# Decay's and gate's running sums as VectorE scans instead of TensorE products, in a one-core hybrid decoder layer

## The chip, the cores and the metric

The kernel runs on one core of one Trainium2 chip. The metric is the device time of one execution in microseconds (us), as a median over runs. The engines are named TensorE (PE in the profile; PEld are its weight loads), VectorE (DVE), ScalarE (ACT), GpSimd (POOL) and SyncE (SP, here the queue from which nearly all DMAs are issued).

## The reference

One decoder layer over 4096 tokens of width 1024. A modulated RMSNorm output h feeds one input projection; its columns go to three parallel mixers (sliding-window attention, RWKV-7, gated linear attention, "GLA"), each is multiplied by a SiLU gate path, and one output projection, a norm and a gate follow. The change is in how two mixers get their decays, cut here to that:

```python
# RWKV-7: per token and channel, state S of each 64-wide head
w = -softplus(-(w0 + tanh(xw @ w1) @ w2)) - 0.5
decay = exp(-exp(w))            # = exp(-e^-0.5 * sigmoid(w0 + ...))
S = S * decay[None, :] + sa[:, None] * (kk * a)[None, :] + v[:, None] * k[None, :]
y = S @ r
# GLA, 4 heads with 32 key and 64 value channels
gk = log_sigmoid((h @ gk1) @ gk2 + gk_b) / 16
b = cumsum(gk)                  # inside a chunk
o = masked((q * exp(b)) @ (k * exp(-b)).T) @ v + (q * exp(b)) @ S
S = exp(b_last) * (S + (k * exp(-b)).T @ v)
```

## The kernel before, in words

Two phases. In the first, 16 blocks of 256 tokens (NT) pass through stages that are written as generators: `stage_a` (norm, hT), `stage_p` (the projections pv, lp, zz, gqk), `stage_d` (named "w": gate and decay), `stage_qa`, `stage_qb`, `stage_qc` (RWKV's triangular systems inside a chunk and their inverse), `stage_v`, `stage_k`, `stage_r` (GLA's products), `stage_q2` (RWKV's chain of states, four chunks of 64 tokens a block), and `stage_c` and `stage_g`, which prepare the second phase's weights. The second phase does attention, gates and the output projection. Results of the first pass through DRAM (hscr, mscr).

The code's order comes from `emit`, which picks the stream whose inputs are ready first. `Order` records every step with an estimated cost and its dependencies, and `pin` lays the steps of each engine out in a fixed order: the step of lowest rank that is ready, on TensorE preferring the tiling of the array that is set. So all instructions have the line of one helper (`call`, L337), and a group in the profile is known by its tiles. Where a scan is among the steps, `Order.note` has a rate of its own for it in the changed kernel.

The names that matter:
- `gla_gate` (L598): zp is the transpose of the gate's 16 low-rank columns and a column of ones (vg[:, a, 256:273]); zlT its copy; gp the product with gk2 (gk2s); ga and gl the log-sigmoid.
- `stage_d`: cgp are gate's running sums, products of gl with a triangular table CTG that is counted from the middle of the 128 tokens; cgc, egp, egm their clamp and exponentials; gmax the largest sum met, for a flag that selects another path. uw is the tanh of the low-rank decay input, wps its product with w2 (w2s) plus w0, which comes in by extra bf16 products (one16 with w0p); aps the same for the rate a; gw and ta their tanh. cw are decay's running sums, products of gw with the table CT, also counted from a chunk's middle; ep and em their exponentials, 65 positions a chunk; cd and em0 what carries a state to the next chunk's and the next block's reference.
- `stage_q2`: Sst is the state, rescaled by em0 at a block's start (L1504). `stage_r`: Gpk and Gst are GLA's state, packed and spread.
- PSUM banks have tags. cw takes "at" and "tr", which the other stages' products use too; cgp takes "m".

The TensorE products in single precision run in two passes each, and small ones are laid on parts of the array: 64*64 means 64 rows by 64 columns.

Of the kernel before, what the change touches and what calls it, by code (L numbers as in the profile page):

```python
# [21 lines left out]
P = 128  # L22
D = 1024
T = 4096
NT = 256
# [5 lines left out]
GATE_LIMIT = 30.0  # L31
# [33 lines left out]
class Order:  # L65
# [34 lines left out]
    def note(self, eng, name, outs, ins, func, r):  # L100
# [44 lines left out]
        else:  # L145
# [256 lines left out]
def hybrid_kernel(ctx, tc, x, xc, rows, ada1, adaw, w1, wl, w2, wo, cst, abias, out):  # L402
# [238 lines left out]
    bdm, gk2s, sinks = kept[:, 0:256], kept[0:17, 256:384], kept[:, 384:392]  # L641


    with ExitStack() as p1:

        soon = ("tables", "scolb", "uw", "w0p0", "w0p1", "one16", "mu_s", "mu_c", "a0h")
        late = ("td", "tf0", "tf1", "Sst0", "Sst1", "lnx")
        tags = ("gvh", "gvl", "xh", "b1", "gl", "bl", "cs", "ch", "gw", "zs", "gaw", "gacc", "zl0", "zl1", "zl2", "early",
                "zb1", "ta", "em", "ep", "zb0", "b2", "zb2", "kg", "kt", "egm", "egp", "qg", "vg", "c2", "middle",
                "AS", "osb", "c3", "KB", "ATm", "c1", "RA", "UV", "BK", "cd", "em0", "bon", "ysb", "rs", "Ss", "lasts")  # L650
# [43 lines left out]
        tables = pp.tile([P, 771], F32, name="tables")  # L694
        masks = pp.tile([P, 3 * P + 32], F32, name="masks")
        w2s, a2s, w0s = tables[0:HD, 0:256], tables[:, 0:256], tables[0:HD, 256:512]
        CT, CTG = tables[:, 512:642], tables[:, 642:771]
# [169 lines left out]
        w0p = [pp.tile([HD, 256], BF16, name=f"w0p{j}") for j in range(2)]  # L867
        one16 = pp.tile([HD, HD], BF16, name="one16")
        V.memset(one16, 1.0)
        for j in range(2):  # L870
            V.tensor_copy(w0p[j], w0s)
            V.tensor_tensor(w0s, w0s, w0p[j], op=ALU.subtract)
            V.tensor_scalar(w0p[j], w0p[j], ident[0:HD, j : j + 1], None, op0=ALU.mult)
        V.tensor_add(w0p[0], w0p[0], w0p[1])
        V.scalar_tensor_tensor(w0p[1], w0s, ident[0:HD, 2:3], w0p[0], op0=ALU.mult, op1=ALU.add)
# [5 lines left out]
        gmax = cp.tile([P, 1], F32, name="gmax")  # L881
        G.memset(gmax, 0.0)
# [171 lines left out]
        def stage_p(i):  # L1054
# [56 lines left out]
            for b in range(2):  # L1111
# [5 lines left out]
            V.scalar_tensor_tensor(qg, gqk[:, 0:NT].rearrange("p (a n) -> p a n", a=2), gq_s, e["egp"][:, :, 1:129],  # L1117
                                   op0=ALU.mult, op1=ALU.mult)
            V.scalar_tensor_tensor(kg, gqk[:, NT : 2 * NT].rearrange("p (a n) -> p a n", a=2), Wt["gqk"][2],
                                   e["egm"][:, :, 1:129], op0=ALU.mult, op1=ALU.mult)  # L1120

        def stage_d(i):
# [7 lines left out]
            yield from gla_gate(vg, b1([17, NT], "zlT"), b1([P, NT], "ga"), gl, mt)  # L1130
            yield [gl, "m"]
# [3 lines left out]
            egp = wt([P, 2, 129], "egp", 2)  # L1135
            egm = wt([P, 2, 129], "egm", 2)
            e["egp"], e["egm"] = egp, egm
            cg3 = cgp[:, :258].rearrange("p (a n) -> p a n", a=2)
            cgc = wt([P, 2, 129], "cgc", tag="gl")
            V.tensor_scalar(cgc, cg3, -40.0, 40.0, op0=ALU.max, op1=ALU.min)  # L1140
            gm2 = st.tile([P, 2], F32, tag="gm2", name="gm2")
# [27 lines left out]
            yield [gw, "m", "tr"]  # L1169
            ep = wt([P, 2, 4, 65], "ep", 1)  # L1170
            em = wt([P, 2, 4, 65], "em", 1)
            e["ep"], e["em"] = ep, em
# [9 lines left out]
            joint(False)  # L1182
# [7 lines left out]
            em0 = wt([P, 2, 1], "em0", 2)  # L1190
            e["cd"], e["em0"] = cd, em0
# [16 lines left out]
        def stage_qa(i):  # L1208
# [18 lines left out]
            ta, ep, em = e["ta"], e["ep"], e["em"]  # L1227
# [14 lines left out]
            ems_ = em.rearrange("p b c n -> p (b c) n")[:, :, 1:65]  # L1242
# [139 lines left out]
        def stage_r(i):  # L1382
# [30 lines left out]
            for a in range(2):  # L1413
# [3 lines left out]
                V.scalar_tensor_tensor(heads4[0], now.rearrange("p (o n) -> p o n", o=1).to_broadcast([P, 4, HD]),  # L1417
# [647 lines left out]
    with tc.If(flag == 0):  # L2065
# [7 lines left out]
        with tc.For_i(0, NS, 1) as iv:  # L2073
# [5 lines left out]
            for a in range(2):  # L2079
                PE.transpose(pM[:, a * P : (a + 1) * P], fg[:, 0, a * P : (a + 1) * P], ident)  # L2080
# [159 lines left out]
```

## Time and profile before

| | |
|---|---|
| median of 3 runs | 2008.36 us (2005.95 to 2013.02) |
| profiled execution | 2010.31 us, span 2008.2 us, mean granted TensorE clock 0.989 |
| TensorE busy | 1915.3 us (95%), 24899 instructions |
| weight loads | 1481.6 us (74%) |
| VectorE busy | 1498.6 us (75%), 4246 instructions |
| ScalarE busy | 1130.5 us (56%) |
| GpSimd busy | 311.9 us (16%) |
| DMA | 258.77 MB, mean 129 GB/s |

A group's row in the profile reads: line, engine, operation, written tile <- read tiles, shapes, count, and then busy us and mean ns of one; the idle time just before these instructions stands last, with what ended it. A matmul's length contains its latency, so lengths of neighbours overlap. The first phase's last projection starts at 946.8 us, and both phases' work is interleaved for some 70 us behind it.

### The profile page before, as it was taken

The numbers are of one execution on the slowest core, as the hardware profiler recorded it, in microseconds if no ns is written. First come the engines' busy times: TensorE is split into PE (matmuls) and PEld (weight loads), VectorE is DVE, ScalarE is ACT, GpSimd is POOL, SyncE is SP. The second block draws the span as 40 slices with busy tenths as digits, with TensorE's granted clock in tenths as the row PEclk, the third lists the DMA queues.
The fourth block names the chain that finished last, engine by engine and source line by source line (L and its number), as shares of the span: only waits on it lengthen the run. The fifth ranks groups of instructions, "written<-read, shape, count | busy, mean of one in ns | idle before, by whom it ended". The sixth has DMA issues, their size and how long they took to land.

```text
span 2008.2 us, 59922 instructions
## 1 busy us (share of the span) xinstructions
PE 1915.3 (95%) x24899; PEld 1481.6 (74%) x24899; DVE 1498.6 (75%) x4246; ACT 1130.5 (56%) x2609; POOL 311.9 (16%) x485
## 2 busy tenths in 40 slices
PE   5899999999999999999999999999999999999997
PEld 2677777778787778877777677877778777787683
DVE  5777877788778887777658876777767777677866
ACT  5877777767867665665435445444444444444543
POOL 0622223342122222222100000000000000000001
PEclk8899999999999999999999999999999999999999
DMA  9465444443324421125234433344333443334405
GB/s 375 141 199 171 135 139 152 142 143 108 126 82 126 152 64 62 57 82 168 83 134 135 162 104 106 113 150 130 109 108 110 147 130 116 108 107 143 130 27 178
DMA packets 154267, 258.77 MB, mean 129 GB/s; under 512 B 49026, under 2 KB 100738, under 8 KB 147716
## 3 DMA queue, kind: packets, MB, share of 16 engines
q1 hardware_dynamic: 153844, 254.34, 39.0%
q8 instruction: 198, 3.24, 0.7%
q14 instruction: 81, 0.66, 0.1%
q10 hardware_dynamic: 144, 0.52, 0.1%
HBM read 193.98 MB, written 60.82 MB: 127 GB/s over the span
## 4 chain that ended last, share of the span: by engine, by line
PE 59%; DVE 19%; ACT 8%; DMA 7%; issue 3%; SPq 2%; POOL 1%; DVEq 0%; ACTq 0%; POOLq 0%
PE gp L337 16%; PE op L337 12%; PE zz L337 6%; PE qp L337 4%; PE lp L337 2%; PE pv L337 2%; PE kp L337 2%; PE sc L337 2%; DVE q L337 2%; PE ovp L337 2%; DVE mtp L337 2%; SPq L337 2%; DMA cs<-in_wo 2%; DVE pr L337 1%; DMA cs<-in_w 1%
## 5 line engine op out<-in xcount | busy, mean ns | idle before, releaser
L337 PEld LDWEIGHTS <-mtp 128*128 128x128 f16 x1344 | 130.2, 98 | 144.7 <-issue 4.4
L337 PE MATMUL op<-o,mtp 128*128 128x512 f16 x768 | 172.3, 379 | 0.0
L337 ACT ACTIVATE pr<-pr,nm,lsc 128x256 f32<-128x256 f32 (+1 forms) x256 | 149.1, 584 | 16.4 <-DVE nm L337 16.4
L337 PE MATMUL op<-ov,mtp 128*128 128x512 f16 x576 | 142.9, 379 | 3.4 <-DVE yv L337 2.1
L337 PEld LDWEIGHTS <-hT 128*128 128x128 f16 x1536 | 117.1, 98 | 20.5 <-issue 2.8
L337 ACT ACTIVATE mtp<-yv,oi 128x1024 f16<-128x1024 f32 x30 | 34.5, 1150 | 155.1 <-DVE yv L337 114.3
L337 DVE CUSTOM_DVE_ANT_0 pr<-sc,ab,kept 128x256 f32<-128x256 f32 (+1 forms) x256 | 108.0, 475 | 14.7 <-PE sc L337 14.4
L337 POOL TENSOR_TENSOR ry<-sy,expo 128x1 f32<-128x1 f32 x30 | 19.1, 638 | 587.8 <-DVE sy L337 587.8
L337 DVE TENSOR_TENSOR yv<-op,yv 128x512 f32<-128x512 f32 x105 | 70.3, 681 | 47.2 <-PE op L337 33.4
L337 PE MATMUL pv<-gvh,hT 128*128 128x272 f16 x512 | 98.8, 283 | 3.9 <-ACT hT L337 2.4
L337 DVE SCALAR_TENSOR_TENSOR ag<-ag,gp 128x512 f32<-128x512 f32 x64 | 43.3, 676 | 75.2 <-ACT ag L337 75.2
L337 PE MATMUL zz<-hT,rh 128*128 128x256 f16 x512 | 93.4, 279 | 0.8 <-DVE zb L337 0.8
L337 ACT ACTIVATE ag<-gp,gh 128x512 f32<-128x512 f32 x64 | 43.6, 682 | 89.5 <-PE gp L337 89.5
L337 PE MATMUL zz<-hT,kh 128*128 128x256 f16 x512 | 92.4, 273 | 0.0
L337 PE MATMUL lp<-hT,Lh 128*128 128x256 f16 x512 | 91.4, 276 | 0.1
L337 PE MATMUL gqk<-hT,gqkh 128*128 128x256 f16 x512 | 87.7, 273 | 0.1
L337 PE MATMUL qp<-hT,q0h 128*128 128x256 f16 x512 | 86.5, 274 | 1.1 <-DVE ag L337 1.1
L337 PE MATMUL zz<-hT,vh 128*128 128x256 f16 x512 | 87.3, 273 | 0.0
L337 PE MATMUL gp<-hT,q5h 128*128 128x256 f16 x512 | 86.5, 274 | 0.5 <-DVE p2e L337 0.5
L337 PE MATMUL gp<-hT,q3h 128*128 128x256 f16 x512 | 86.0, 273 | 0.9 <-DVE q L337 0.9
L337 PE MATMUL qp<-hT,q1h 128*128 128x256 f16 x512 | 85.8, 272 | 0.3 <-DVE kT L337 0.3
L337 PE MATMUL gp<-hT,q4h 128*128 128x256 f16 x512 | 86.1, 273 | 0.0
(442 smaller groups left out, 5850.7 us busy)
## 6 DMA issues: line engine op xcount, KB each, us to landing
ov<-woscr SPq DMA_DIRECT2D x96, 512.0 KB, 4.2
xh<-in_x SPq DMA_DIRECT2D x32, 512.0 KB, 4.4
xt<-in_xc SPq DMA_DIRECT2D x16, 1024.0 KB, 8.1
hscr<-hT SPq DMA_DIRECT2D x16, 1024.0 KB, 5.1
hT<-hscr SPq DMA_DIRECT2D x16, 1024.0 KB, 4.8
x<-in_x SPq DMA_DIRECT2D x30, 512.0 KB, 4.4
out<-yv SPq DMA_DIRECT2D x30, 512.0 KB, 2.9
cs<-in_w SPq DMA_DIRECT2D x56, 256.0 KB, 3.7
```

Of the source, the lines that this page charges most:

```text
L337: r = f(*args, **kw)
```

## The change

Both running sums are taken along the free axis by VectorE's `tensor_tensor_scan` with channels on partitions, and all references are moved from the middle to the start of a chunk.

- The gate: the transpose takes 128 columns (vg[:, a, 145:273]) and the product is one of 128 x 128 by 256 with a zero-padded gk2, so gp and gl have channels on partitions. Two scans of 128 tokens write egp; gmin keeps the smallest sum; a floor at -1024; both exponentials read egp. cgp, its table, the clamp and the reductions go.
- The decay: w2s is the stationary side and uw the moving one, so wps has channels on partitions, and w0 comes in as the bias of two tanh halves. One scan over 512 elements, with a tile `reset` that is zero at each chunk's first token, sums gw in place; ep (a lasting tile with a column of ones) and em read it. The cw products and the table go.
- em0 and its rescaling of the state go; cd is one copy. In `stage_r` the state's steps lose their em-like factor.
- The constants shrink: `tables` from 771 to 256 columns. `Order.note` gives a scan 2.08e-3 us an element.

```diff
     def gla_gate(vg, zlT, ga, gl, tile_of):
-            PE.transpose(zp[:17, a * P : (a + 1) * P], vg[:, a, 256:273], ident)
-        V.tensor_copy(zlT, zp[:17, :NT])
+            PE.transpose(zp[:, a * P : (a + 1) * P], vg[:, a, 145:273], ident)
+        V.tensor_copy(zlT, zp[:, :NT])
...
-        for a in range(2):
-            for h in range(2):
-                PE.matmul(gp[64 * h : 64 * h + 64, a * P : (a + 1) * P], zlT[:, a * P + 64 * h : a * P + 64 * h + 64], gk2s,
-                          start=True, stop=True)
+        PE.matmul(gp[:, :NT], gk2s, zlT, start=True, stop=True)
...
     def stage_d(i):
...
-            cgp = mt("cgp")
+            egp = wt([P, 2, P], "egp", 2)
+            egm = wt([P, 2, P], "egm", 2)
             for a in range(2):
-                PE.matmul(cgp[:, a * 129 : (a + 1) * 129], gl[:, a * P : (a + 1) * P], CTG, start=True, stop=True)
...
-            V.tensor_scalar(cgc, cg3, -40.0, 40.0, op0=ALU.max, op1=ALU.min)
-            V.tensor_reduce(gm2, cg3[:, :, 0:129:128].rearrange("p a n -> p n a"), axis=AX.X, op=ALU.max)
-            V.tensor_tensor(gmax, gmax, gm2[:, 0:1], op=ALU.max)
-            V.tensor_reduce(gm2, cg3[:, :, 0:129:128].rearrange("p a n -> p n a"), axis=AX.X, op=ALU.min)
-            V.scalar_tensor_tensor(gmax, gm2[:, 1:2], -1.0, gmax, op0=ALU.mult, op1=ALU.max)
-            S.activation(egp, cgc, AF.Exp)
-            S.activation(egm, cgc, AF.Exp, scale=-1.0)
+                V.tensor_tensor_scan(egp[:, a], ones, gl[:, a * P : (a + 1) * P], 0.0, op0=ALU.mult, op1=ALU.add)
+                V.tensor_tensor(gmin, gmin, egp[:, a, P - 1 : P], op=ALU.min)
+            V.tensor_single_scalar(egp, egp, -16 * 64.0, op=ALU.max)
+            S.activation(egm, egp, AF.Exp, scale=-1.0 / 16.0)
+            S.activation(egp, egp, AF.Exp, scale=1.0 / 16.0)
...
-                    PE.matmul(wps[hs, cols], one16, w0p[1], start=True, stop=False)
-                    PE.matmul(wps[hs, cols], uw[:, n * P + 64 * h : n * P + 64 * h + 64], w2s, start=False, stop=True)
+                    PE.matmul(wps[hs, cols], w2s[:, n * P + 64 * h : n * P + 64 * h + 64], uw, start=True, stop=True)
...
-            S.activation(gw, wps.rearrange("p (a n) -> p a n", a=2), AF.Tanh, scale=0.5)
-            V.tensor_scalar(gw, gw, 1.0, -0.5 * EM05, op0=ALU.add, op1=ALU.mult)
+            for b in range(2):
+                S.activation(gw[:, b], wps[:, b * NT : (b + 1) * NT], AF.Tanh, scale=0.5, bias=w0h[:, b : b + 1])
+            V.tensor_scalar(gwf, gwf, 1.0, -0.5 * EM05, op0=ALU.add, op1=ALU.mult)
+            V.tensor_tensor_scan(gwf, reset, gwf, 0.0, op0=ALU.mult, op1=ALU.add)
...
-            cw = [pst(tag, "cw")[:, 0:260] for tag in ("m", "tr")]
-            joint()
-            for b in range(2):
-                for a in range(2):
-                    for h, hs in enumerate(half):
-                        for c, cs in enumerate(half):
-                            PE.matmul(cw[c][hs, (2 * b + a) * 65 : (2 * b + a + 1) * 65],
-                                      gw[cs, a, b * P + 64 * h : b * P + 64 * h + 64], CT[cs, 65 * c : 65 * c + 65],
-                                      start=True, stop=True)
-            for c in range(2):
-                for t, sg in ((ep, 1.0), (em, -1.0)):
-                    S.activation(t.rearrange("p b (a c) n -> p c (b a) n", c=2)[:, c], cw[c].rearrange("p (g n) -> p g n", g=4),
-                                 AF.Exp, scale=sg)
+            S.activation(ep.rearrange("p b c n -> p (b c) n")[:, :, 1:65], gw4, AF.Exp)
+            S.activation(em.rearrange("p b c n -> p (b c) n"), gw4, AF.Exp, scale=-1.0)
...
-            V.tensor_mul(cd[:, :, 0:3], ep[:, :, 0:3, 64], em[:, :, 1:4, 0])
-            V.tensor_copy(cd[:, :, 3:4], ep[:, :, 3, 64:65])
-            V.tensor_copy(em0, em[:, :, 0, 0:1])
+            V.tensor_copy(cd, ep[:, :, :, 64])
...
     def stage_r(i):
-                V.scalar_tensor_tensor(heads4[0], now.rearrange("p (o n) -> p o n", o=1).to_broadcast([P, 4, HD]),
-                                       egm[:, a, 0:1], heads4[1], op0=ALU.mult, op1=ALU.mult)
+                V.tensor_tensor(heads4[0], now.rearrange("p (o n) -> p o n", o=1).to_broadcast([P, 4, HD]), heads4[1], op=ALU.mult)
+                V.tensor_scalar(then, now, egp[:, a, P - 1 : P], None, op0=ALU.mult)
...
     def stage_q2(i):
-                if c == 0 and i > 0:
-                    V.tensor_tensor(Sc, Sc, em0.to_broadcast([P, 2, HD]), op=ALU.mult)
-                    yield [Sc, "sq"]
```

TensorE's order in the middle of the first phase (block 11 of the 16 is in `stage_d`), before: the decay sums cw stand among the projection's zz products, beside the state's sp and yp and GLA's kvp.

```order
L337 LDWEIGHTS kh
L337 MATMUL zz<-hT,kh 128x256
L337 MATMUL cw<-tables,gw 64x65 x16
L337 MATMUL sp<-UV,BK 64x64 x4
L337 MATMUL yp<-UV,AT 64x64 x4
L337 MATMUL kvp<-vg,kt 32x64 x4
L337 LDWEIGHTS kh
```

The same engine around that block's wps products now; they are the stage's last on TensorE.

```order
L339 MATMUL zz<-hT,kh 128x256
L339 MATMUL aps<-x_11367,tables 64x256
L339 MATMUL wps<-uw,tables 64x256
L339 MATMUL aps<-x_11367,tables 64x256
L339 MATMUL wps<-uw,tables 64x256
L339 MATMUL aps<-x_11367,tables 64x256
L339 MATMUL wps<-uw,tables 64x256
L339 MATMUL aps<-x_11367,tables 64x256
L339 MATMUL wps<-uw,tables 64x256
L339 MATMUL atp<-RA,KB 64x128 x16
L339 MATMUL up<-rs,tf_515 64x64 x4
L339 LDWEIGHTS kl
```

The w0p products that stood between the wps ones and the cw group are gone, and other blocks' 64-row groups (atp, up) stand behind wps instead.

VectorE's order for the gate in a block of the middle, before: clamp and reductions of cgp, with other stages' steps among them (ch is a split weight, bon the bonus term).

```order
L337 COPY rs<-rp 128x128
L337 TENSOR_SCALAR cgc<-cgp 128x258
L337 TENSOR_REDUCE gm_11931<-cgp 128x2
L337 SCALAR_TENSOR_TENSOR ch<-cs,wo_sc,ch 128x4x128
L337 TENSOR_TENSOR gmax<-gmax,gm_11931 128x1
L337 TENSOR_REDUCE gm_11931<-cgp 128x2
L337 SCALAR_TENSOR_TENSOR gmax<-gm_11931,gmax 128x1
L337 TENSOR_TENSOR bon<-bp,zb_11319 128x256 x2
```

And now; a scan is printed as a SCALAR_TENSOR_TENSOR (egp<-first,gl and, a few rows below, gw<-reset,gw).

```order
L339 COPY Xs<-Xp 32x256 x2
L339 SCALAR_TENSOR_TENSOR egp<-first,gl 128x128
L339 SCALAR_TENSOR_TENSOR x_11367<-lp,ivL,bl 128x256
L339 TENSOR_TENSOR gmin<-gmin,egp 128x1
L339 SCALAR_TENSOR_TENSOR egp<-first,gl 128x128
L339 SCALAR_TENSOR_TENSOR ch<-cs,wo_sc,ch 128x4x128
L339 TENSOR_TENSOR gmin<-gmin,egp 128x1
L339 TENSOR_SCALAR egp<-egp 128x256
```

The two scans stand where clamp and reductions stood, and the copies of the inverse's products (Xs<-Xp) and the inputs of other stages have moved to their sides.

SP's order at the end of the first phase, before (q0 to q6 are the second phase's weights, h and l the two halves of a split number; tdr and td the inverse's transfers, osb and ysb results on their way to mscr):

```order
L337 DMA tdr<-TT 64x128 x2
L337 DMA q0h<-wscr 128x2048
L337 DMA td<-tdr 16x8x16 x3
L337 DMA mscr<-osb 128x512
L337 DMA td<-tdr 16x8x16 x5
L337 DMA q0l<-wscr 128x2048
L337 DMA q1h<-wscr 128x2048
L337 DMA mscr<-ysb 128x512
L337 DMA q1l<-wscr 128x2048
L337 DMA q3h<-wscr 128x2048
```

And now:

```order
L339 DMA q0h<-wscr 128x2048
L339 DMA q0l<-wscr 128x2048
L339 DMA q5h<-wscr 128x2048
L339 DMA q5l<-wscr 128x2048
L339 DMA q1h<-wscr 128x2048
L339 DMA mscr<-ysb 128x512
L339 DMA mscr<-osb 128x512
L339 DMA tdr<-TT 64x128 x2
L339 DMA q1l<-wscr 128x2048
L339 DMA td<-tdr 16x8x16 x8
L339 DMA q3h<-wscr 128x2048
```

The loads of q0 and q1h have moved ahead of block 14's tdr and td; q1l and q3h stand behind tdr as before. TensorE's order has moved with it: behind the last gqk product stand all four groups of that block's inverse (Xp, Xq, Xp, X), of which two stood ahead of it before.

More of the change, by code (lines that the diff above doesn't have):

```diff
@@ L30 @@
 LN2 = math.log(2.0)
-GATE_LIMIT = 30.0
+GATE_LIMIT = 16 * 60.0
 HOP, VL, AL, PL = 0.4, 0.2, 0.2, 0.06
@@ L153, in note @@
                 fixed = 0.09
+            elif name == "tensor_tensor_scan":
+                rate = 2.08e-3
             elif name == "memset":
@@ L640, in hybrid_kernel @@
     kept = cp.tile([P, 392], F32, name="kept")
-    bdm, gk2s, sinks = kept[:, 0:256], kept[0:17, 256:384], kept[:, 384:392]
+    bdm, gk2s, sinks = kept[:, 0:256], kept[:, 256:384], kept[:, 384:392]
     with ExitStack() as p1:
-        soon = ("tables", "scolb", "uw", "w0p0", "w0p1", "one16", "mu_s", "mu_c", "a0h")
+        soon = ("tables", "scolb", "uw", "reset", "w0h", "mu_s", "mu_c", "a0h")
         late = ("td", "tf0", "tf1", "Sst0", "Sst1", "lnx")
         tags = ("gvh", "gvl", "xh", "b1", "gl", "bl", "cs", "ch", "gw", "zs", "gaw", "gacc", "zl0", "zl1", "zl2", "early",
-                "zb1", "ta", "em", "ep", "zb0", "b2", "zb2", "kg", "kt", "egm", "egp", "qg", "vg", "c2", "middle",
-                "AS", "osb", "c3", "KB", "ATm", "c1", "RA", "UV", "BK", "cd", "em0", "bon", "ysb", "rs", "Ss", "lasts")
+                "zb1", "ta", "em", "zb0", "b2", "zb2", "kg", "kt", "egm", "egp", "qg", "vg", "c2", "middle",
+                "AS", "osb", "c3", "KB", "ATm", "c1", "RA", "UV", "BK", "cd", "bon", "ysb", "rs", "Ss", "lasts")
         wk1 = {n: pool_of(p1, f"work1{n}", 1) for n in tags}
@@ L692, in half_tile @@
             return t
-        tables = pp.tile([P, 771], F32, name="tables")
+        tables = pp.tile([P, 256], F32, name="tables")
         masks = pp.tile([P, 3 * P + 32], F32, name="masks")
-        w2s, a2s, w0s = tables[0:HD, 0:256], tables[:, 0:256], tables[0:HD, 256:512]
-        CT, CTG = tables[:, 512:642], tables[:, 642:771]
+        w2s, a2s = tables[0:HD], tables
         rmask, gmask, tdelta, tmask = [masks[:, n * P : min((n + 1) * P, 3 * P + 32)] for n in range(4)]
@@ L866, in hybrid_kernel @@
         uw = pp.tile([HD, NT], F32, name="uw")
[L867 to L875, printed above, removed]
+        ep = pp.tile([P, 2, 4, 65], F32, name="ep")
+        V.memset(ep.rearrange("p b c n -> p (b c) n")[:, :, 0:1], 1.0)
+        reset = pp.tile([P, 2 * NT], F32, name="reset")
+        V.memset(reset, 1.0)
+        V.memset(reset[:, 0 : 2 * NT : HD], 0.0)
+        w0h = pp.tile([P, 2], F32, name="w0h")
+        V.tensor_single_scalar(w0h, vcol("w0"), 0.5, op=ALU.mult)
         tfs = [pp.tile([P, 8, HD], F32, name=f"tf{j}") for j in range(2)]
@@ L880, in hybrid_kernel @@
         G.memset(td, 0.0)
-        gmax = cp.tile([P, 1], F32, name="gmax")
-        G.memset(gmax, 0.0)
+        gmin = cp.tile([P, 1], F32, name="gmin")
+        G.memset(gmin, 0.0)
         def piece(src, at):
@@ L1116, in stage_p @@
             e["qg"], e["kg"] = qg, kg
[L1117 removed]
+            V.scalar_tensor_tensor(qg, gqk[:, 0:NT].rearrange("p (a n) -> p a n", a=2), gq_s, e["egp"],
                                    op0=ALU.mult, op1=ALU.mult)
             V.scalar_tensor_tensor(kg, gqk[:, NT : 2 * NT].rearrange("p (a n) -> p a n", a=2), Wt["gqk"][2],
[L1120 removed]
+                                   e["egm"], op0=ALU.mult, op1=ALU.mult)
         def stage_d(i):
@@ L1129, in stage_d @@
             gl = wt([P, NT], "gl", 1)
[L1130 to L1147 removed]
+            yield from gla_gate(vg, b1([P, NT], "zlT"), b1([P, NT], "ga"), gl, mt)
+            yield [gl]
+            egp = wt([P, 2, P], "egp", 2)
+            egm = wt([P, 2, P], "egm", 2)
+            e["egp"], e["egm"] = egp, egm
+            for a in range(2):
+                V.tensor_tensor_scan(egp[:, a], ones, gl[:, a * P : (a + 1) * P], 0.0, op0=ALU.mult, op1=ALU.add)
[3 more added lines that the diff above has]
+            S.activation(egp, egp, AF.Exp, scale=1.0 / 16.0)
             yield [("x1", i)]
@@ L1424, in stage_r @@
                 joint(False)
-                V.scalar_tensor_tensor(then, now, egm[:, a, 0:1], kvp[:, 0:HD], op0=ALU.mult, op1=ALU.add)
-                V.tensor_scalar(then, then, egp[:, a, 128:129], None, op0=ALU.mult)
+                V.scalar_tensor_tensor(then, kvp[:, 0:HD], egp[:, a, P - 1 : P], then, op0=ALU.mult, op1=ALU.add)
                 yield [Gc, qb[a], "at"]
@@ L1493, in stage_q2 @@
             yield [("qc", i), ("v", i)]
-            UV, AT, RA, cd, em0, bon, tf = [e[n] for n in ("UV", "AT", "RA", "cd", "em0", "bon", "tf")]
+            UV, AT, RA, cd, bon, tf = [e[n] for n in ("UV", "AT", "RA", "cd", "bon", "tf")]
             yield [tf, "sq"]
@@ L2077, in hybrid_kernel @@
                 run(gla_values(fh, Wf, vg, a, pA))
-            run(gla_gate(vg, fz[0:17, 0, :], fz[:, 1, :], fg[:, 0, :], {"zp": pM, "gp": pB}.get))
-            for a in range(2):
-                PE.transpose(pM[:, a * P : (a + 1) * P], fg[:, 0, a * P : (a + 1) * P], ident)
+            run(gla_gate(vg, fz[:, 0, :], fz[:, 1, :], fg[:, 0, :], {"zp": pM, "gp": pB}.get))
             exf = fg[:, 1, :].rearrange("p (a n) -> p a n", a=2)
-            S.activation(fg[:, 1, :], pM[:, :NT], AF.Exp, scale=1.0 / 16.0)
+            S.activation(fg[:, 1, :], fg[:, 0, :], AF.Exp, scale=1.0 / 16.0)
             for b in range(2):
@@ L2162, in _consts @@
     bd = ((i[:, None] // 32) == (np.arange(256)[None, :] // 64)).astype(f)
-    pos = np.arange(65)
-    ctr = np.zeros((P, 2, 65), f)
-    for c in range(2):
-        tt = i - 64 * c
-        inn = (tt >= 0) & (tt < 64)
-        ctr[:, c, :] = np.where(inn[:, None], (tt[:, None] < pos[None, :]).astype(f) - (tt[:, None] < 32).astype(f), 0)
-    posg = np.arange(129)
-    ctg = ((i[:, None] < posg[None, :]).astype(f) - (i[:, None] < 64).astype(f)) / f(16)
     qi = i[:, None]
```

38 lines of the change are left out of this document (18 added, 20 removed).

## The prediction

> **What bounds the kernel now.** I read the busy times by stretch first: the change touches only the stage that runs once per token block (16 blocks), from about 60 to 950 us, so its price is read there. Then what TensorE waited for in that stretch, and then its timeline around the products that go. The columns after a stretch's length are busy times of TensorE, its weight loads, VectorE, ScalarE and GpSimd, the granted clock, the DMA share and rate.
>
> ```profile
> core 0: us, PE busy (x) PEld busy (x) DVE busy (x) ACT busy (x) POOL busy (x), PEclk, DMA share, GB/s
> 0.00:60.00 60.00, 37.14 (x202) 18.16 (x203) 33.10 (x126) 34.15 (x63) 9.34 (x25) 0.91 0.98 368
> 120.00:900.00 780.00, 756.92 (x12403) 612.63 (x12401) 621.70 (x1939) 556.89 (x1216) 217.09 (x338) 1.00 0.38 118
> 900.00:980.00 80.00, 77.33 (x1306) 60.89 (x1305) 56.26 (x201) 36.23 (x84) 16.75 (x26) 0.94 0.40 134
> 980.00:1060.00 80.00, 74.98 (x1064) 62.73 (x1063) 48.78 (x167) 31.70 (x84) 6.41 (x7) 0.98 0.35 115
> PE yt L337 <- DVE ysb L337: 4.5, 4, 1.7
> ...
> PE cgp L337 <- DVE gl L337: 2.3, 3, 1.2
> ...
> PE cw L337 <- DVE tsc L337: 0.5, 1, 0.5
> ```
>
> Between 120 and 900 us TensorE is busy 756.92 of 780 us (97%), at full clock, while VectorE has 158 us free (20%) and ScalarE 223 us. The waits of TensorE (total, times, longest) are many and small: the first row is the largest total from 60 to 980 us, 4.5 us in four waits. So this stretch is a queue of TensorE work that always has something to run, and a microsecond of TensorE work taken away should shorten it by nearly that much. Before 60 us DMA sets the pace (0.98 busy).
>
> **TensorE: what goes.** The timeline gives start, length and count; the price is the distance from a group's start to the next group's, since the lengths overlap. Behind it stand the weight loads of the full-width sums (shortest, median, longest ns) and all decay sums of 60 to 980 us (busy us, mean ns of one, idle time before).
>
> ```profile
> 526.24 0.38 PE L337 MATMUL zz<-hT,kh 128*128 128x256 f16 x2
> 526.55 0.70 PE L337 MATMUL cw<-tables,gw 64*64 64x65 f32 x32
> 527.07 0.41 PE L337 MATMUL up<-rs,tf 64*64 64x64 f32 x8
> ...
> 585.02 0.68 PE L337 MATMUL cw<-tables,gw 64*64 64x65 f32 x31
> 585.64 0.28 PE L337 MATMUL zz<-hT,rh 128*128 128x256 f16 x1
> ...
> 571.11 0.61 PE L337 MATMUL cgp<-tables,gl 128*128 128x129 f32 x4
> 571.56 0.27 PE L337 MATMUL lp<-hT,Lh 128*128 128x256 f16 x1
> ...
> 523.16 0.39 PE L337 MATMUL wps<-tables,uw 64*64 64x256 f32 x2
> 523.38 0.29 PE L337 MATMUL wps<-w0p,one 64*64 64x256 bf16 x2
> 523.49 0.39 PE L337 MATMUL wps<-tables,uw 64*64 64x256 f32 x2
> ...
> 508.25 0.65 PE L337 MATMUL gp<-kept,zlT 17*64 17x128 f32 x8
> 508.83 0.39 PE L337 MATMUL lp<-hT,Lh 128*128 128x256 f16 x2
> ...
> 506.03 0.38 PE L337 MATMUL zp<-first,vg 128*17 128x128 f32 x2
> 506.25 0.38 PE L337 MATMUL lp<-hT,Lh 128*128 128x256 f16 x2
> ...
> L337 PEld LDWEIGHTS cgp<-tables,gl x64: 186/192/192, 79.1 to 909.5; 128*128 128x128 f32 x64
> ...
> L337 PE MATMUL cw<-tables,gw 64*64 64x65 f32 x512 | 11.2, 222 | 0.5 <-DVE tsc L337 0.5
> ```
>
> - Decay's sums (cw), 32 passes a block: 526.55 to 527.07 is 0.52 us when a group of the same 64*64 tiling follows, 0.62 us (585.02 to 585.64) when a full-width product follows. As a check, 11.2 us busy in 16 blocks is 0.70 us each, and the last 0.18 us of that overlaps. I take 0.52: the 0.1 us that pass before the group starts (two zz products from 526.24 take 0.38 in all where one takes 0.28, so they follow each other by 0.10 to 0.11 and the second has streamed by about 526.45) is the price of changing the tiling, and it goes only where no neighbour needs the same change. Along TensorE's order up to the last gqk product the tiling changes 612 times before and 604 times now: 8 x 0.09 = 0.7 us in all.
> - Gate's sums (cgp), 4 passes: 571.11 to 571.56, 0.45 us.
> - The w0 rows (wps from w0p), 4 products in two pairs of one tile each: 523.38 to 523.49, 0.11 us a pair, 0.21 a block. The bias of the activation replaces them. The swap of uw and w2s between stationary and moving side keeps tile and columns, so nothing.
> - Gate's product: 8 passes of 128 columns on 17*64 tiles take 508.25 to 508.83, 0.58 us with the change back to full width in it. Now 2 passes of 256 columns at full width: 512 columns, as many as cgp's 4 x 129 = 516, so 0.45 us by cgp's row. Saved 0.13; I take 0.10, since some of the tiling change stays with the neighbour ahead.
> - The transposes (zp) stream the same 128 columns: 0.22 us for two. Only their weight load grows from 17 to 128 columns. Nothing is taken; the worst is 0.08 us each (the 0.19 us load not hidden under 0.11 us), 2.6 us in all.
>
> Sum: 16 x (0.52 + 0.45 + 0.21 + 0.10) = 20.5 us, and 0.7 for tilings. The high end, with 0.62, 0.52 and 0.13, is 16 x 1.48 = 23.7; the low end, with the transposes at their worst, 17.9.
>
> **VectorE: what goes and comes.**
>
> ```profile
> L337 DVE TENSOR_REDUCE gm<-cgp x32: 140/154/163, 80.2 to 910.6; 128x2 f32<-128x4 f32 x32
> L337 DVE TENSOR_SCALAR cgc<-cgp x16: 405/418/428, 79.9 to 909.9; 128x258 f32<-128x258 f32 x16
> L337 DVE TENSOR_TENSOR gmax<-gmax,gm x16: 142/158/666, 80.4 to 910.4; 128x1 f32<-128x1 f32 x16
> L337 DVE COPY cd<-ep x16: 138/159/169, 91.9 to 929.4; 128x2 f32<-128x2 f32 x16
> L337 DVE TENSOR_TENSOR Sst<-Sst,em x15: 261/283/1130, 190.7 to 976.8; 128x128 f32<-128x128 f32 x15
> L337 DVE TENSOR_SCALAR rn<-np x32: 406/415/424, 83.5 to 937.0; 128x256 f32<-128x256 f32 x32
> L337 DVE SCALAR_TENSOR_TENSOR ta<-ta,rn x16: 676/683/1530, 93.7 to 945.0; 128x512 f32<-128x512 f32 x16
> L337 POOL TENSOR_TENSOR qb<-qg,kept 128x512 f32<-128x512 f32 x32 | 36.1, 1149 | 46.4 <-DVE qg L337 46.3
> ```
>
> The columns are the shortest, median and longest ns. Out, by medians: the clamp 0.42, two reductions 0.31, the two gmax steps 0.32, three small decay copies and products 0.48 by the cd row, the em0 scaling of the state 0.28: 1.81 us a block. In: two running minima 0.32, one floor over 256 columns (at most the 0.42 of a 256-column row), one small copy 0.16, and three scans: one of 512 elements, two of 128. No row shows a scan. Below, it costs what a two-operand pass costs: 0.68 for 512 and 0.28 for 128. Above, the slowest row of 512 elements with two operands, GpSimd's 1.15, and a quarter of that, 0.29, for 128. So 1.24 to 1.73 for the three, and 0.3 to 0.8 us a block added, 5 to 13 us in all. The scan is nearest to VectorE's own 0.68 row, as it reads two streams on that engine; I take 0.3. It is costed at nothing on the path: the 158 us free on VectorE cover it. If that cover is gone (the scan stands ahead of an eviction that TensorE needs), up to 13 us come back; that is a rival below.
>
> [...]
>
> **ScalarE, GpSimd and the queues.**
>
> ```profile
> L337 ACT ACTIVATE gw<-wps x16: 575/582/592, 83.3 to 917.1; 128x512 f32<-128x512 f32 x16
> L337 ACT ACTIVATE ta<-aps,a0h x32: 453/464/497, 83.8 to 917.6; 128x256 f32<-128x256 f32 x32
> L337 ACT ACTIVATE ep<-cw x32: 368/389/406, 88.6 to 926.1; 128x260 f32<-128x260 f32 x32
> L337 ACT ACTIVATE rn<-rn x16: 629/630/634, 86.6 to 939.2; 128x512 f32<-128x512 f32 x16
> tables<-in_cst SPq DMA_DIRECT2D x1, 385.5 KB, 9.9
> L337 PE MATMUL yt<-first,ysb x64: 272/273/476, 195.0 to 1021.0; 128*128 128x128 f32 x64
> L337 PE MATMUL op<-ov,mtp x576: 376/379/390, 1075.0 to 1997.1; 128*128 128x512 f16 x192
> SPq L337 <- ACT osb L337: 13.0, 1, 13.0
> ```
>
> ScalarE does the first tanh in two halves with a bias (2 x 0.46 for 0.58) and the exponentials in two pieces of 512 for four of 260 (2 x 0.63 for 4 x 0.39): +0.34 and -0.30 us, level, under 223 us of free time. GpSimd keeps its work. The bank that cw held beside the attention and gate products is not asked for any more; I count nothing for it. The table load shrinks from 771 to 256 columns, 0.26 MB less in the DMA-bound start: 0.7 us at 368 GB/s (0 to 0.7). VectorE's eight set-up steps for w0 lie beside that DMA time and count nothing.
>
> The end of the stage is where I give some back. Behind the last gqk product the new order still holds one block's Xp, Xq, Xp, X round entire (before, its first half was done) and block 15's np and atp groups; the last yt stands some 140 TensorE rows deeper. On SP's queue q0 and q1h, loads of the second stage into the slots of the projections' weights, now stand ahead of block 14's tdr and td, so the inverse's transfers wait there for those slots, and TensorE's Xp behind them. The cover is the second stage's q and gate products; the first op product starts at 1075.0, 54 us behind the last yt at 1021, so the loads for it have room. TensorE idles 2.67 + 5.02 = 7.7 us in 900 to 1060; I add a quarter of that, 2 us (0 to 7.7).
>
> Sum: -20.5 - 0.7 - 0.7 + 2 = -19.9 us. The profiled execution took 2010.3 us (span 2008.2), 1.9 above the median of the three runs: 1990.4 on its scale, 1988.5 as a median.
>
> **Rivals.**
> 1. More than forecast: with cw's bank free, cgp's and cw's waits gone and no em0 step in the chain of states, half of the 23.1 us idle of 120 to 900 goes too, with the high end of the sum: 2008.4 - 23.7 - 1.4 - 11.5 = 1972. For it: the waits named above. Against: they total 3 us of the waits, and other waits will take the holes.
> 2. VectorE pays back: scans at their upper bound, felt by TensorE in full, as they stand in VectorE's order ahead of evictions: 1988.5 + 13 = 2001.5. For it: VectorE is busy 80% and the scans have no other engine. Against: 20% free. [...]
> 3. No change to measure: the blocks' rate is set by a chain over engines (state step, transfers between the inverse's steps), and the TensorE time comes back as idle time: 2008.4 - 0.7 = 2007.7. Against: such a chain would show as long waits of TensorE before the chain's products, and the largest total of the stretch is 4.5 us.
> 4. Slower: at the change of stages SP waits in order, once for 13.0 us already, on osb. With q0 and q1h ahead of block 14's tdr and td, the inverse and all that hangs on it (block 15's round, its states, its yt) comes later by such waits, and TensorE idles once its second-stage products are used up. It decides from 28 us of new idle time on (22 saved, 6 to be seen), over two waits of 13.0 without cover; three give 2008.4 - 22 + 39 = 2025. Against: 54 us of products lie behind the last yt now and can move ahead of it.
>
> **Numbers.** Three runs before spread by 7 us; 0.3% (6 us, 2002.3 to 2014.4) is about what can be told from no change. Chances: forecast (1979 to 1996) 0.53, rival 1 0.10, rival 2 (1996 to 2004) 0.21, rival 3 0.10, rival 4 0.06. Faster holds the first two and most of the third: 0.80; same 0.13; slower 0.07. The range leaves out part of rival 1 and rivals 3 and 4: 1977 to 2004.
>
> **What would show it.** Right: no cw and cgp rows; gp as 2 passes with about 0.45 us to its follower; TensorE busy some 20 us less up to the last gqk and its idle time there still near 3%; the last gqk product some 20 us earlier. Wrong: waits of TensorE on egp, gw or on evictions behind a scan of several us in total (rival 2); idle time of 900 to 1060 us well over 8 us, with SP waiting ahead of tdr or td (rival 4); scans over 1.2 us; zp's distance to its follower near 0.4 us.

## The result, and the profile after

The changed kernel takes 2027.8 us (median of 4 runs, 2026.0 to 2039.0) against 2010.7 for the kernel before: a ratio of 1.0099, 95% interval 1.0078 to 1.0120. It is slower by 17 us. The forecast was 1988.5, range 1977 to 2004. The profiled execution of the changed kernel took 2026.0 us, its span is 2024.2 (before: 2008.2).

The stretches of the first table, now:

```profile
core 0: us, PE busy (x) PEld busy (x) DVE busy (x) ACT busy (x) POOL busy (x), PEclk, DMA share, GB/s
120.00:900.00 780.00, 738.50 (x11521) 588.00 (x11518) 627.58 (x1902) 556.50 (x1194) 214.10 (x331) 0.99 0.38 117
900.00:980.00 80.00, 74.28 (x1244) 58.89 (x1241) 51.07 (x157) 34.65 (x75) 16.27 (x28) 0.98 0.45 151
980.00:1060.00 80.00, 72.74 (x1088) 58.15 (x1089) 50.38 (x196) 31.85 (x90) 10.84 (x13) 0.98 0.34 109
```

Between 120 and 900 us TensorE is busy 18.4 us less (756.92 to 738.50). In a window of fixed length that is 18.4 us more idle time in any case (23.1 to 41.5), and the changed kernel, some 10 us behind at the window's end, has done less of its work there. So the better count runs from 60 us to the start of the last gqk product, the same projections in both: TensorE is busy 843.5 us instead of 852.7 and idle 53.6 us instead of 34.1. The busy time fell by 9.2 us, and 19.5 us of idle time came. In the window VectorE is busy 5.9 us more.

The rows by shape say where the stages stand (shortest, median, longest ns; first and last start):

```profile
L339 DVE TENSOR_TENSOR_SCAN gw<-reset,gw x16: 1201/1218/1626, 85.5 to 945.3; 128x512 f32<-128x512 f32 x16
L339 DVE TENSOR_TENSOR_SCAN egp<-first,gl x32: 392/420/1274, 76.7 to 922.4; 128x128 f32<-128x128 f32 x32
L339 PE MATMUL gqk<-hT,gqkl x256: 272/273/283, 88.1 to 957.1; 128*128 128x256 f16 x128
L339 PE MATMUL yt<-first,ysb x64: 272/273/330, 195.2 to 1041.9; 128*128 128x128 f32 x64
L339 PE MATMUL op<-ov,mtp x576: 377/380/391, 1090.9 to 2012.8; 128*128 128x512 f16 x192
```

The last gqk product starts at 957.1 instead of 946.8 (+10.3). The first op product starts at 1090.9 instead of 1075.0 (+15.9), so 5.6 us more are lost between the two. From there to the last op product it is 921.9 us, and 922.1 before. All of the loss lies ahead of 1091 us, two thirds of it in the blocks.

TensorE's waits from 60 to 980 us are still many and small; no new one stands out, and none of the largest is directly on a scan's output:

```profile
PE kp L339 <- DVE KB L339: 3.7, 1, 3.7
PE vp L339 <- DVE zb L339: 3.5, 3, 2.9
PE Xp L339 <- DVE D L339: 3.0, 4, 1.3
PE wssp L339 <- ACT gqkh L339: 2.9, 1, 2.9
PE pv L339 <- issue: 2.9, 1, 2.9
PE yt L339 <- DVE ysb L339: 2.8, 4, 1.1
```

### The profile page after: what moved, and what is told of

It is laid out like the page before. It is cut to its first block, busy times and chain, and to the rows that moved or that the text cites. A ratio compares the mean times of both kernels' runs of the same rounds, so it can differ in the third digit from the quotient of the medians.

```text
span 2024.2 us, 58396 instructions
## 1 busy us (share of the span) xinstructions
PE 1908.3 (94%) x24163; PEld 1463.7 (72%) x24163; DVE 1510.4 (75%) x4210; ACT 1133.6 (56%) x2593; POOL 313.2 (15%) x485
## 4 chain that ended last, share of the span: by engine, by line
PE 48%; DVE 17%; ACT 5%; DMA 3%; issue 3%; POOL 1%; SPq 1%; ACTq 0%; DVEq 0%; POOLq 0%
PE gp L339 16%; PE op L339 12%; PE qp L339 4%; PE zz L339 3%; PE sc L339 2%; DVE mtp L339 2%; PE ovp L339 2%; DVE q L339 2%; PE kp L339 2%; DVE pr L339 2%; PE pv L339 1%; DMA cs<-in_wo 1%; PE lp L339 1%; POOL yr L339 1%; DVE tsc L339 1%
## 5 line engine op out<-in xcount | busy, mean ns | idle before, releaser
L339 PEld LDWEIGHTS <-hT 128*128 128x128 f16 x1536 | 120.3, 100 | 30.7 <-issue 7.9
L339 PE MATMUL pv<-gvh,hT 128*128 128x272 f16 x512 | 103.1, 294 | 6.6 <-ACT hT L339 3.9
L339 PE MATMUL gp<-hT,q6h 128*128 128x256 f16 x512 | 85.0, 273 | 0.0
```

The lines of the kernel that those rows point to most:

```text
L339: r = f(*args, **kw)
```

## The experiments

Three questions: do the scans cost the time; is a microsecond of TensorE work worth a microsecond in this stretch; and how much does the written order alone move the time? Ratios are to runs of the kernel before on the same chip, whose medians were 2008.4 to 2011.1 us.

### The scans away, the order kept

In the changed kernel each scan is issued as a plain product of its inputs. The planner still counts a scan, so every engine's order stays as it was. The running sums are left out.

```diff
         f = getattr(self.eng, name)
+        if name == "tensor_tensor_scan":
+            f = lambda out, d0, d1, first, op0, op1: self.eng.tensor_tensor(out, d0, d1, op=op0)
```

> The changed kernel with its orders kept as they are, but each of the 48 scans replaced by a two-operand product of the same tiles (the sums are left out). The scans took 1.22 us (512 elements) and 2 x 0.42 us (128); products should take 0.68 and 2 x 0.28, so VectorE gets 16 x 0.82 = 13 us back, in place. Theory 'scans' (their time or length is what the blocks wait for): 2028 falls by 8 to 13 us, to 2015 to 2020. Theory 'order' (the new fixed order of the engines is a worse one, whatever the scans cost): 2023 to 2029. Theory 'chain' (a chain over engines through decay and gate sets the rate of blocks): the chain holds the scans, so as 'scans'.

Measured: 2027.1 us (ratio 1.0085, 1.0059 to 1.0111), as the changed kernel itself. Its row:

```profile
120.00:900.00 780.00, 738.69 (x11525) 589.06 (x11523) 620.01 (x1902) 556.31 (x1193) 212.27 (x332) 0.99 0.37 117
```

VectorE is 7.6 us less busy and nothing came of it. What the scans take beyond plain products is not the loss: rival 2 falls. The products in their place still take 1.25 us a block; that part was not taken away.

### Work away, the order kept

Now the kernel before. A step can be recorded for the planner and not issued, so that all other instructions keep their order:

```diff
-            r = f(*args, **kw)
+            r = NOT_ISSUED if kw.pop("left_out", False) else f(*args, **kw)
```

First the decay products and the w0 rows, that is, the larger part of what the change itself takes from TensorE (the exponentials then read gw itself):

```diff
-                    PE.matmul(wps[hs, cols], one16, w0p[1], start=True, stop=False)
+                    PE.matmul(wps[hs, cols], one16, w0p[1], start=True, stop=False, left_out=True)
...
-                                      start=True, stop=True)
+                                      start=True, stop=True, left_out=True)
```

> The kernel before with its orders kept, but the 512 decay products (cw) and the 64 w0 products are not issued on TensorE; the exponentials read gw itself instead (the decay's running sums and w0 are left out). By the prediction's rows that is 16 x (0.52 + 0.21) = 11.7 us of TensorE work, out of the same order. 'A microsecond of TensorE work saved shortens the stretch by nearly that much': 2010.7 - 9 to 12, so 1999 to 2002. Theory 'chain': the blocks keep their rate, 2006 to 2011. If 'order' holds, the first number comes here, although the real change did not bring it.

Measured: 2010.5 us (1.0009, 0.9993 to 1.0026). No gain. The row:

```profile
120.00:900.00 780.00, 746.26 (x11848) 599.56 (x11847) 619.82 (x1936) 558.65 (x1216) 216.67 (x338) 1.00 0.38 118
```

TensorE's busy time fell by 10.7 us; the forecast's 0.73 us a block makes about 10 for the 14 blocks of this window. The price was right, and at an equal time in all, the work came back as idle time. This is the forecast's main step tried by itself, without a scan and without a new order, and it fails.

Then a dose seven times as large, on TensorE alone:

```diff
-    def proj(po, W, c0, cw, hT):
+    def proj(po, W, c0, cw, hT, thin=False):
...
-                PE.matmul(po, a[:, k, c0 : c0 + cw], hT[:, b, k, :], start=(n == 0), stop=(n == 3 * KD - 1))
+                PE.matmul(po, a[:, k, c0 : c0 + cw], hT[:, b, k, :], start=(n == 0), stop=(n == 3 * KD - 1),
+                          left_out=thin and b == 1)
```

> The kernel before with its orders kept, but one of the three passes of each zz product (the low half of hT; 768 passes of 256 columns, 0.108 us each by their spacing) is not issued: 83 us of TensorE work less, out of the same order, all in the first phase. Theory 'TensorE bound after all' (11.7 us was too small a dose to see): 2010 - 70 to 83, so 1927 to 1940. Theory 'chain' (the rate is set by a path that goes through all engines, on which TensorE holds 373 of 780 us and zz 107): at most a third of zz's 107 us, 36, and less as the next path is near: 1980 to 2005.

Measured: 2010.3 us (1.0003, 0.9987 to 1.0019). 83 us of TensorE work are worth nothing that can be measured:

```profile
120.00:900.00 780.00, 709.31 (x11879) 558.91 (x11878) 621.96 (x1939) 556.05 (x1217) 219.06 (x341) 0.99 0.37 117
```

One reservation: the mean granted clock of its ten runs was 0.983, against 0.990 in the runs of before on that chip. 0.007 of 2008 us is 14, so by this estimate up to some 14 of the 83 us may have been gained and lost again to the clock.

The same on VectorE, then both:

```diff
-                                op=ALU.mult)
-                V.tensor_reduce(TT[:, :, t : t + 1], tsc[:, :, 0 : t + 1], axis=AX.X, op=ALU.add)
+                                op=ALU.mult, left_out=1 < t < 15)
+                V.tensor_reduce(TT[:, :, t : t + 1], tsc[:, :, 0 : t + 1], axis=AX.X, op=ALU.add, left_out=1 < t < 15)
```

> The kernel before with its orders kept, but 26 of the 30 small VectorE steps a block that invert the 16-wide triangles (tsc, TT; the steps for t = 2 to 14) are not issued: 416 steps, 0.285 and 0.223 us long in the mean, 106 us of VectorE work less, all in the first phase, and out of a serial piece of the blocks' chain. Theory 'VectorE bound': 2009 - 80 or more, under 1930. Theory 'one path' (the chain of waits of before, on which tsc and TT hold 23 us): 1985 to 1995. Theory 'many paths of like length' (taking one engine's work away leaves the others): 1998 to 2011.

> Both at once, orders kept: the 768 zz passes (83 us of TensorE) and the 416 small VectorE steps (106 us) are not issued. Theory 'many paths of like length': where either alone gave little, both give clearly more than their sum, 1950 to 1990, as the chain of waits without the zz passes lay on VectorE for 303 us, 68 of them on tsc and TT. Theory 'a bound elsewhere' (SP's queue, DMA, ScalarE): again 1998 to 2011.

Measured: 2006.8 us (0.9984, 0.9971 to 0.9997) and 2000.1 us (0.9956, 0.9944 to 0.9969). VectorE's steps alone gave some 3 us, as "many paths" had it. Both together were expected at 1950 to 1990 and gave some 9 us: that size was wrong.

ScalarE next, by issuing the logarithms as Identity, which saves changes of function table (64 loads of 1.283 us each from 60 to 980 us before; ScalarE's busy time from 120 to 900 us falls from 556.89 to 485.01); then all three:

```diff
+            issued = [AF.Identity if a is AF.Ln and self.model.order.first else a for a in args]
-            r = NOT_ISSUED if kw.pop("left_out", False) else f(*args, **kw)
+            r = NOT_ISSUED if kw.pop("left_out", False) else f(*issued, **kw)
```

> The kernel before with its orders kept, but the first phase's logarithms on ScalarE are issued as Identity (the logarithms are left out), so that the function table is loaded 3 times and not 67: 64 loads of 1.283 us, 82 us of ScalarE's time. Theory 'many paths of like length': the table loads hold 15 us of the chain of waits of before; 0 to 10 us less, 1999 to 2010. Theory 'ScalarE sets the rate': 60 us or more less, under 1950.

> All three at once, orders kept: 83 us of TensorE, 106 of VectorE and 82 of ScalarE not issued, in a first phase of 900 us. Theory 'many paths over three engines': now clearly less, 1930 to 1980. Theory 'something on no engine's work' (transfers, SyncE's queue, buffers): 1990 to 2000, as with two of them.

Measured: 1999.0 us (0.9932, 0.9912 to 0.9953) and 1981.7 us (0.9862, 0.9838 to 0.9885). ScalarE's 82 us are worth the most, some 13, a little more than expected; all 271 us together are worth 28, where 30 to 80 were expected. The row with all three left out:

```profile
120.00:900.00 780.00, 722.00 (x12182) 570.74 (x12181) 574.66 (x1638) 492.80 (x1181) 218.28 (x347) 0.99 0.38 120
```

The 28 us are a tenth of the sum of 271, which one chain through all the work taken away would have given back, and a third of 82, the smallest of the three, which three engines side by side would have given if their work set the rate. So no one engine sets the rate of the blocks, but neither do the three by their work: most of what was taken away came back as waiting.

### Less work, a new order

The same work left out so that the planner does not see it and writes all orders anew: the zz passes alone, and all three.

```diff
             for a, b in ((whi, 0), (whi, 1), (wlo, 0)):
+                if thin and b == 1:
+                    n += 1
+                    continue
...
-            for t in range(1, 16):
+            for t in (1, 15):
```

(the second edit, and Identity for the logarithms, in the run with all three)

> The kernel before without the 768 zz passes, this time with the orders written anew by its planner, which does not see them. If the planner can turn TensorE's free time into time: 2009 - 40 to 83, 1926 to 1969. Theory 'many paths': the other paths stay as long as they were, 1985 to 2020, the draw of the order (10 us either way) on top.

> The kernel before without the 768 zz passes, without the 416 small VectorE steps and without the first phase's logarithms, as in the run with all three, but with the orders written anew by its planner, which does not see them. Theory 'the fixed orders hold the gain back': well under the 1982 of the kept orders, 1935 to 1965 (the planner's own count of the first phase falls by 53 of 963 us). Theory 'the blocks do not wait for this work': 1972 to 1990.

Measured: 1991.6 us (0.9910, 0.9889 to 0.9930) and 1996.8 us (0.9946, 0.9923 to 0.9970). Both expectations of a large gain were missed. The first gained some 19 of 83 us, where the old order gave none. The second has less work still and is no faster than the first, and 15 us slower than the same work taken out of the old order (1981.7). So "the fixed orders hold the gain back" fits the first pair and not the second. Only one new order was run of each, and orders of the same work differ by up to 23 us (next part): these two runs settle neither the worth of the work nor that of the old order.

### The order alone

The same instructions, with one number of the planner changed, in either kernel; their order changes, and with it the turns of the buffers. One pair changes the rate at which the emission counts VectorE, the others what it counts for handing a tile to another engine:

```diff
-LANES = ((0.06, 1.04e-3, VL), (0.02, 1.0e-3, AL), (0.1, 2.3e-3, 0.0), (0.0, 1e-3 / 2.4, PL), (0.05, 0.0, 2.0))
+LANES = ((0.06, 1.0e-3, VL), (0.02, 1.0e-3, AL), (0.1, 2.3e-3, 0.0), (0.0, 1e-3 / 2.4, PL), (0.05, 0.0, 2.0))
...
-HOP, VL, AL, PL = 0.4, 0.2, 0.2, 0.06
+HOP, VL, AL, PL = 0.5, 0.2, 0.2, 0.06
```

> The changed kernel with one number of its planner changed: the rate at which the emission counts VectorE steps, 1.04 to 1.00 ns an element. The instructions are the same; only their order and the buffers' turns differ. Theory 'order': the time moves by 6 us or more, and likely down, since the planner's own count of the first phase's end falls by 18 of 970 us: 2005 to 2020. Theories 'scans' and 'chain': the same work and the same chain, 2023 to 2031.

> The kernel before with the same one number of the planner changed (1.04 to 1.00 ns an element). Theory 'order', with the order of before a lucky one among its neighbours: slower by 5 to 15 us, 2015 to 2026. Theories 'scans' and 'chain': 2008 to 2013, as the work is the same.

> The changed kernel with another number of its planner changed: what the emission counts for handing a tile to another engine, 0.40 to 0.45 us. The same instructions in another order. Theory 'order': it moves by 5 us or more, and by the planner's own count (958 for 970) down: 2005 to 2020. Theory 'the change itself costs': 2022 to 2032.

> The kernel before with the hand-over counted at 0.45 for 0.40 us. Theory 'order', with before a lucky order: slower, 2015 to 2026 (the planner's own count is 974.5 for 963). Theory 'the change itself costs': 2007 to 2013.

> The changed kernel with the hand-over counted at 0.50 us. Theory 'order': 2000 to 2018 (the planner's own count is 954 for 970), and at best under before's 2010. Theory 'the change itself costs': 2022 to 2032.

> The kernel before with the hand-over counted at 0.50 us, the pair of the changed kernel's run at 0.50 (2004.5). Theory 'order': anywhere from 2010 to 2026. If it is as far above its pair as the prediction had it, 20 us: 2024; if the change is worth nothing in the mean over orders, the four pairs (as handed, rate 1.00, hand-over 0.45 and 0.50) average to no difference: about 2008 to 2024.

> The changed kernel with the hand-over counted at 0.35 us instead of 0.40; another order of the same instructions. Theory 'order': somewhere in 2004 to 2028, as the four orders so far.

> The pair of it: the kernel before with 0.35. Theory 'order': 2008 to 2026, as the four orders so far, with no fixed distance to its pair.

> The changed kernel with the hand-over counted at 0.60 us, a last order. Theory 'order': 1998 to 2022; the planner's own count (953) is as low as that of the run at 0.50 (954), but that count has missed before (958 gave 2027, 952 gave 2019).

Measured, medians in us, and the ratio to the kernel before as handed:

| planner's number | before | after | after less before |
|---|---|---|---|
| as handed (1.04 ns, 0.40 us) | 2010.7 | 2027.8 (1.0099, 1.0078 to 1.0120) | +17.1 |
| rate 1.00 ns | 2023.5 (1.0082, 1.0050 to 1.0115) | 2018.7 (1.0049, 1.0031 to 1.0067) | -4.8 |
| hand-over 0.35 us | 2015.6 (1.0024, 1.0008 to 1.0040) | 2020.6 (1.0050, 1.0028 to 1.0072) | +5.1 |
| hand-over 0.45 us | 2024.6 (1.0079, 1.0059 to 1.0099) | 2026.8 (1.0087, 1.0066 to 1.0109) | +2.2 |
| hand-over 0.50 us | 2017.7 (1.0050, 1.0032 to 1.0069) | 2004.5 (0.9983, 0.9970 to 0.9995) | -13.2 |
| hand-over 0.60 us | not run | 2017.0 (1.0047, 1.0030 to 1.0064) | |

Before as handed is the fastest of its five orders; after as handed is the slowest of its six, level with that at 0.45. The means of the five pairs are 2018.4 and 2019.7: a difference of 1.3 us, with a standard deviation of 11 between pairs, so about 14 either way at 95%. The change's own worth, taken over orders, cannot be told from nothing here. That its 17 us are mostly the distance between a lucky and an unlucky order fits these runs best, as 17 lies outside that interval; how much of it is the change itself, five pairs cannot say. The planner's own count, on which the expectations of single orders leaned, was a poor guide: it put the orders at 0.45 and 0.50 four microseconds apart, and they are 22 apart on the chip.

Of the versions that leave nothing out, the changed kernel at 0.50 is the only one that beats both: the kernel before by 0.17% (0.05 to 0.30%). Its row has the idle time of the blocks at 36.2 us and the clock at 1.00:

```profile
120.00:900.00 780.00, 743.79 (x11665) 596.50 (x11660) 641.08 (x1923) 562.71 (x1206) 218.59 (x334) 1.00 0.38 119
```

## Why the prediction was wrong, point by point

**"A microsecond of TensorE work taken away should shorten it by nearly that much."** This is the step that failed. Taken in the old order, 11.7 us gave nothing and 83 us gave nothing that can be measured. It rested on TensorE being busy 756.92 of 780 us, with only small waits. A matmul's recorded length contains its latency (an f16 pass of 256 columns is recorded at 0.273 us and follows its like by 0.109), so gaps of up to some 0.16 us between matmuls count as busy. A better measure from the same records: for each matmul, take the distance to the next start, but no more than the median distance between two of its own kind (the same tiles and shape, or the same shape where no two of the same tiles follow each other). In 120 to 900 us of the kernel before that sums to 548 of 780 us; in 1100 to 1900, where the second phase runs, to 762 of 800. The busy times show both stretches as almost full; only the second one is.

The chain of waits gave a warning. For the whole run it reads:

```profile
PE 59%; DVE 19%; ACT 8%; DMA 7%; issue 3%; SPq 2%; POOL 1%; DVEq 0%; ACTq 0%; POOLq 0%
```

Its pieces between 120 and 900 us, added up by engine, give TensorE 373 of 780 us, VectorE 196, ScalarE 82, transfers 65, queues or issue 52 and GpSimd 10. All 512 cw passes together hold about 4 us of that path. And it is only one path: followed back from the last gqk product in the run without the zz passes, it lies, from 120 us on, 303 us on VectorE and 236 on TensorE.

**The order.** The forecast priced the moved instructions at 0.7 us of tilings and 2 us at the end. The runs put a redrawn order at 2004 to 2028 for one and the same set of instructions. How such a loss looks: around 438 us of the changed kernel TensorE stands at vp, which wait for zb (starts, lengths, idle time before):

```profile
437.69 0.38 PE L339 MATMUL rb<-first,rsx 128*128 128x128 f32 x2
440.97 0.33 PE L339 MATMUL vp<-first,zb 128*128 128x128 f32 x1 [2.90 <-DVE zb L339]
441.65 0.55 PE L339 MATMUL vp<-first,zb 128*128 128x128 f32 x3 [0.35 <-DVE zb L339]
...
442.33 0.66 PE L339 MATMUL pv<-gvh,hT 128*128 128x272 f16 x2
442.78 0.43 PE L339 MATMUL pv<-gvl,hT 128*128 128x272 f16 x1
...
445.67 0.40 PE L339 MATMUL pv<-gvh,hT 128*128 128x272 f16 x2
445.90 0.28 PE L339 MATMUL pv<-gvl,hT 128*128 128x272 f16 x1
```

VectorE, meanwhile, does this in its own order:

```profile
438.19 0.68 DVE L339 SCALAR_TENSOR_TENSOR RA<-rn,ep 128x512 f32<-128x512 f32 x1
438.79 0.68 DVE L339 SCALAR_TENSOR_TENSOR ta<-ta,rn 128x512 f32<-128x512 f32 x1
439.39 0.35 DVE L339 TENSOR_TENSOR tsc<-TT,AS 128x120 f32<-128x120 f32 x1
439.66 0.67 DVE L339 TENSOR_TENSOR KB<-ta,em 128x512 f32<-128x512 f32 x1
440.26 0.26 DVE L339 TENSOR_REDUCE TT<-tsc 128x8 f32<-128x120 f32 x1
440.45 0.47 DVE L339 SCALAR_TENSOR_TENSOR zb<-zz,mu_c,zs 128x256 f32<-128x256 f32 x1
```

Without a gap, five steps of other stages stand ahead of zb, and none of them is a scan. ScalarE had finished zs, which zb reads, by 437.9 us. The same 2.9 us wait stands in the run without scans. And the wait has a second price: two pv passes take 0.45 us at 442.33 and 0.23 at 445.67, as the clock shows:

```profile
438.00:442.00 4.00, 0.75 (x5) 0.49 (x5) 4.00 (x12) 0.49 (x2) 3.15 (x3) 1.00 0.25 66
442.20:445.60 3.40, 3.40 (x17) 2.27 (x16) 3.37 (x7) 2.56 (x6) 2.65 (x5) 0.50 0.11 26
446.00:454.00 8.00, 8.00 (x129) 6.77 (x128) 3.20 (x6) 7.12 (x17) 0.00 (x0) 1.00 0.08 7
```

After the idle 3 us TensorE is granted half its clock for 3.4 us, 1.7 us lost. The trace's record of the clock has one such stretch from 120 to 900 us before and four after; from 60 to 900 us the loss is 6.8 us before and 13.7 after, from 900 to 1060 it is 6.8 and 3.4. So up to 7 of the 10 us that the blocks lost may be this second price. One wait does not decide it: ahead of the stretch at 735.7 us after stand two waits of 0.90 and 1.42 us (TensorE busy 1.08 of 3.4 us), and in the run without the zz passes a wait of 2.92 us at 597.4 has no half clock behind it. Over the eleven profiled runs that leave nothing out, the loss between 60 and 1060 us lies between 8.5 and 29.0 us and rises with the span (correlation 0.77), so this price is a good part of what parts one order from another, or goes along with it.

**The sizes.** TensorE's prices hold where a run tests them: the cw and w0 rows by the run without them, and the new transposes still follow their like by 0.109 us. For the whole sum there is no clean test, since up to the last gqk product TensorE's busy time fell by 9.2 us with some 7 us more lost at half clock. The changes of tiling fell from 612 to 566 in the traces, not to 604. The scans were mis-sized: 1.218 and 0.420 us against 0.68 and 0.28 taken, above even my upper ends of 1.15 and 0.29, so "1.24 to 1.73 for the three" is 2.06. Between 128 and 512 elements a scan grew by 2.08 ns an element ((1218 - 420) / 384), where VectorE's two-operand steps of the same sizes in the same trace grew by 1.04 (k<-k,zb at 682 and Ss<-sp,Sst at 283 ns, medians). Their extra length cost nothing that the run without scans could find.

**The end.** Taken at 2 us, measured at 5.6. Block 15's inverse does come some 22 us later, 10 of which are the blocks' own delay, and the last yt starts at 1041.9 instead of 1021.0. As rival 4 had it, SyncE's queue, ahead of block 14's tdr and td, stands at q0h and then at q1h until zz products are done (10.1 and 6.3 us; in total, times, longest):

```profile
SPq L339 <- PE zz L339: 16.5, 2, 10.1
```

But TensorE's idle time in 900 to 1060 grew only from 7.7 to 13.0 us, as it had other products to run. Rival 4's place was right and its price was not.

**The rivals.** Rival 3, "the blocks' rate is set by a chain over engines", had a chance of 0.10 and named what the runs in the old order show: "the TensorE time comes back as idle time". "Such a chain would show as long waits of TensorE" was the wrong test, since gaps of up to some 0.16 us do not show in that view. No rival had a worse order as such, which by the pairs is what most likely decided the sign.

**Open.** What the blocks wait for, when 271 us of work on three engines are gone and 28 us of time with them, is not settled. The depth of the buffers and SyncE's queue were not tried.

## What to carry to other kernels

Before a saving on the "busy" engine is counted, add up what the matmuls need by their spacing, and sum the chain of waits by engine for that stretch: work is worth time only on that path, and only until the next path. Where a planner fixes the order of every engine, an edit also redraws that order; run the old and the new kernel under several neighbouring orders before a difference of 1% is put down to the edit. A wait of some 3 us on TensorE can cost more than its own length: in the traces of the kernel before and of the changed one, TensorE was idle for 2.2 us or more (up to 3.72) ten times between 60 and 1060 us, and each time a stretch at half clock (nine in all, 3.4 or 10.2 us long) began at most 1.6 us before or after the end of the wait; the wait of 2.92 us in the run without the zz passes had none.

## What was not expected of the hardware

- TensorE at half clock (0.50) for 3.4 us behind a wait of 2.90 us, in the changed kernel from 442.2 us on.
- Taking much TensorE work away in the old order lowered its granted clock. The mean over the runs was 0.983 without the 83 us, 0.985 with VectorE's steps out as well and 0.986 with all three, against 0.990 for the kernel before on the same chips; where only VectorE's or only ScalarE's work was out, it stayed at 0.990 and 0.991. In the profiled run without the 83 us, half-clock stretches cost 22.2 us between 60 and 1060 us, against 13.7 before (6.8 with the small dose of 11.7 us). A saving that turns into idle time can be partly eaten in this way. A new order can do as much with nothing left out (up to 29.0 us, the changed kernel at 0.45), so the 30.7 and 29.0 us of the two kernels with less work and a new order cannot be put down to the work:

```profile
120.00:900.00 780.00, 726.74 (x12014) 568.92 (x12007) 572.75 (x1615) 484.22 (x1159) 217.22 (x341) 0.97 0.37 116
```

This is the run with all three kinds of work left out and a new order: 53.3 us idle, and a clock of 0.97 where the kernel before had 1.00.
